# A depthwise convolution moved wholly to TensorE, by column tiles and shifted copies

## The chip, the cores and the metric

The kernel runs on one core of a Trainium2 chip. The metric is the device time of one execution in microseconds; the median of three runs is given. The program is one launch that computes three transformer blocks for 256 positions of width 1024.

## What is computed

The change touches one step of the first block, the mixer with a convolution branch. Cut to that (`S` = 256, 512 channels, 31 taps, float32):

```python
def conformer_conv(u, glu_b, dw_w, dw_b, ln_g, ln_b):
    u = u + glu_b
    a, g = jnp.split(u, 2, axis=-1)
    h = a * jax.nn.sigmoid(g)
    h = jnp.pad(h, ((0, 0), (30, 0), (0, 0)))
    h = lax.conv_general_dilated(             # depthwise: each channel with its own 31 taps
        h, dw_w[:, None, :], window_strides=(1,), padding='VALID',
        dimension_numbers=('NWC', 'WIO', 'NWC'), feature_group_count=512)
    h = layer_norm(h + dw_b, ln_g, ln_b)      # over the channels
    return jax.nn.silu(h)

# first block
h = rms_norm(x, norm1_g)
q, k, v, u = jnp.split(h @ w_in, [512, 1024, 1536], axis=-1)
q, k = rope(rms_norm(q)), rope(rms_norm(k))   # 8 heads of 64
attn = causal_attention(q, k, v)
x = x + jnp.concatenate([attn, conformer_conv(u, ...)], -1) @ w_out
x = x + swiglu(rms_norm(x))                   # width 2816
```

Two more blocks of the same size follow (other attentions, two feed-forward parts each). They are not touched.

## The kernel before, in words

**Tiling.** The 256 positions are two tiles of 128 rows (`t` = 0, 1). All weights are streamed from HBM once, in blocks of mostly 1 MB in the order of `PLAN`. `load` asks for a block into one of three `raw` buffers, on SP's queue. `split` turns it into a rounded high part on ScalarE (L242) and the remainder on VectorE (L243); the parts of four blocks fit in the pool `hl`. Each weight product is three matmuls, high by high, high by low, low by high (`mm3`, L272 to L274). Eight banks of PSUM hold four `mm` tiles, two for attention and two for transposes. `take` hands out the next block and asks for later loads and splits ahead of it.

**The first mixer** (`mixer1`). The first four weight blocks give the two halves of `u`. The gated product is transposed, and `hc[c]` holds chunk `c` of 128 channels by 30 zeros and 256 positions (L701). Then come the query block, the key block (blocks 4 to 7), the scores with softmax, lambda (a small value for the second part), the value block (8 and 9), `attend`, the norm of the convolution, and the output projection `w_out` (10 to 13). For queries and keys, ScalarE sums the squares of each head (L754), POOL takes the power (L285), VectorE does the rotary step in five operations (L531 to L535, last multiply L767), TensorE transposes (L520).

**The convolution** before is divided. Chunks 0 and 1 and the first 12 taps of chunk 2 are done on VectorE: one multiply-add of 128x256 for each tap (L731, L733), 74 in all, drawn in four portions between the other steps (`bg`). The remaining 19 taps of chunk 2 and all 31 of chunk 3 are matmuls on TensorE (L721): the stationary operand is a 128x128 diagonal of tap weights, made on the host and loaded four taps at a time on SP's queue (`dg`, two buffers, L716), the moving one a shifted slice of `hc`. The norm (L788 to L803) takes all four chunks by transposes.

**Order.** The program is written once in the order of the code, and a planner puts each engine's instructions in a fixed order: by their place in the code, but by its own estimate of when operands and buffers are ready. On the chip each engine keeps that order, and waits where something isn't ready yet. SP issues the DMAs in such an order too. Each DMA there waits until the one that used its semaphore before has landed; there are eight in turn.

Of the kernel before, what the change touches and what calls it, by code (L numbers as in the profile page):

```python
# [7 lines left out]
F32 = mybir.dt.float32  # L8
F32R = mybir.dt.float32r
BF16 = mybir.dt.bfloat16  # L10
AF = mybir.ActivationFunctionType
ALU = mybir.AluOpType
AX = mybir.AxisListType

P = 128
# [15 lines left out]
FIRST_SPLIT = 512  # L31
SLOTS = 25
E_BUFS = 9
DG_BUFS = 2
HP = 150
HP2 = 100
CONV_DVE = (31, 31, 12, 0)
BG = (10, 10, 24, 20)

# [82 lines left out]
C_DWB = 72  # L124
C_DWW = 76
# [50 lines left out]
class K:  # L176
    def __init__(self, tc, aps, pools):
        self.tc, self.nc = tc, tc.nc
        self.w, self.x_in, self.cols_in, self.rows_in, self.sh_in, self.rev_in, self.dg_in, self.out = aps
        (self.cp, self.raw, self.hl, self.sl, self.xp, self.gp, self.sm, self.psm, self.pst) = pools  # L180
        self.blk = []
        self.nload = self.nsplit = self.nuse = 0
        off = 0
        self.offs = []
        for b in PLAN:
            self.offs.append(off)
            off += P * b[3] * b[5]
        self.uid = 0
# [475 lines left out]
    def mixer1(self, nxt):  # L664
        nc = self.nc
        glu = self.row_bcast(R_GLU, 1024)
        qk = self.slot()
        for j, (r, sw) in enumerate(((R_QN, 0), (R_QN, 1), (R_KN, 0), (R_KN, 1))):
            o = qk[:, j * 64 : (j + 1) * 64]
# [19 lines left out]
        hc = [self.slot() for _ in range(4)]  # L689
        for c in range(4):  # L690
            nc.gpsimd.memset(hc[c][:, 0:30], 0.0)
        for t in range(2):
            r = self.rstd[t][:, 0:1]
            a, g = self.slot(), self.slot()
            nc.vector.scalar_tensor_tensor(a, pa[t], r, glu[:, :512], op0=ALU.mult, op1=ALU.add)
            nc.vector.scalar_tensor_tensor(g, pg[t], r, glu[:, 512:], op0=ALU.mult, op1=ALU.add)
            nc.scalar.activation(g, g, AF.Sigmoid)
            nc.vector.tensor_tensor(a, a, g, op=ALU.mult)
            tp = self.transpose4(a)
            for c in range(4):  # L700
                nc.scalar.activation(hc[c][:, 30 + t * P : 30 + (t + 1) * P], tp[:, c * P : (c + 1) * P], AF.Copy)  # L701

        w = lambda c, k: self.cols[:, C_DWW + c * 31 + k : C_DWW + c * 31 + k + 1]
        cps = {}

        def conv_pe(c):
            ks = list(range(CONV_DVE[c], 31))
            if not ks:
                return
            if not cps:  # L710
                cps["bank"] = self.mmt()
            ps = cps[c] = cps["bank"][:, (c % 2) * 256 : (c % 2 + 1) * 256]
            for g in range(0, len(ks), 4):
                dg = self.sl.tile([P, 512], F32, tag="dg", name=self.nm("dg"), bufs=DG_BUFS)
                nk = len(ks[g : g + 4])
                nc.sync.dma_start(  # L716
                    dg[:, : nk * P].rearrange("p (k m) -> p k m", k=nk),
                    self.dg_in[c, ks[g] : ks[g] + nk].rearrange("k p m -> p k m"))
                for j, k in enumerate(ks[g : g + 4]):
                    d = dg[:, j * P : (j + 1) * P]  # L720
                    nc.tensor.matmul(ps, d, hc[c][:, k : k + 256], start=(k == ks[0]), stop=(k == 30))  # L721

        acc = [self.slot()[:, :256] for _ in range(4)]

        def conv_dve():
            for c in range(4):
                a = acc[c]
                b = self.cols[:, C_DWB + c : C_DWB + c + 1]
                for k in range(CONV_DVE[c]):
                    if k == 0:  # L730
                        nc.vector.tensor_scalar(a, hc[c][:, 0:256], w(c, 0), b, op0=ALU.mult, op1=ALU.add)  # L731
                    else:
                        nc.vector.scalar_tensor_tensor(a, hc[c][:, k : k + 256], w(c, k), a, op0=ALU.mult, op1=ALU.add)  # L733
                    yield

        it = conv_dve()

        def bg(n):
            for _ in range(n):
                next(it, None)  # L740


        ops = []
        for which in range(2):
            bg(BG[which])
            ps = self.project()
            dst = [self.slot(), self.slot()]
            for t in range(2):
                r = self.rstd[t][:, 0:1]
                sq = self.slot()  # L750
                ss = self.small(8, "qss")
                for h in range(8):
                    c = slice(h * 64, (h + 1) * 64)
                    nc.scalar.activation(sq[:, c], ps[t][:, c], AF.Square, accum_out=ss[:, h : h + 1])  # L754
                r2 = self.small(1, "r2")
                nc.vector.tensor_scalar(r2, r, r, 1.0 / 64, op0=ALU.mult, op1=ALU.mult)
                ms = self.small(8, "qms")
                nc.vector.tensor_scalar(ms, ss, r2[:, 0:1], EPS, op0=ALU.mult, op1=ALU.add)
                f = self.small(8, "qf")
                self.rpow(f, ms)  # L760
                f2 = self.small(8, "qf2")
                nc.vector.tensor_scalar(f2, f, r, 0.125 if which == 0 else 1.0, op0=ALU.mult, op1=ALU.mult)
                q = self.slot()
                a = tabs[t]
                self.rope(ps[t], a[:, which * 128 : which * 128 + 64], a[:, which * 128 + 64 : which * 128 + 128], q, 8, 64)
                qv = q[:, :].rearrange("p (h d) -> p h d", d=64)
                nc.vector.tensor_tensor(qv, qv, f2[:, :].unsqueeze(2).broadcast_to([P, 8, 64]), op=ALU.mult)  # L767
                self.to_T(q, dst, t)
            ops.append(dst)
        sc = self.scores(ops[0], ops[1], lambda h: self.sh[:, H_CAUS : H_CAUS + 256])  # L770
        self.lambda_()
        bg(BG[2])
        v = self.vcopy(self.project())
        conv_pe(3)
        bg(BG[3])
        conv_pe(2)
        att = self.attend(sc, v)
        bg(999)
        for c in range(4):
            if CONV_DVE[c] == 0:  # L780
                nc.scalar.activation(acc[c], cps[c], AF.Identity, bias=self.cols[:, C_DWB + c : C_DWB + c + 1])
            elif c in cps:
                nc.vector.tensor_tensor(acc[c], acc[c], cps[c], op=ALU.add)
        cv = []
        for t in range(2):
            tp = self.tpt()
            for c in range(4):
                nc.tensor.transpose(tp[:, c * P : (c + 1) * P], acc[c][:, t * P : (t + 1) * P], self.ident)  # L788
            st, mv = self.small(6, "bst"), self.small(2, "bmv")
            nc.vector.bn_stats(st, tp)  # L790
            nc.vector.bn_aggr(mv, st)
            ve, rv = self.small(1, "bve"), self.small(1, "brv")
            nc.vector.tensor_scalar(ve, mv[:, 1:2], EPS, None, op0=ALU.add)
            self.rpow(rv, ve)
            xn = self.slot()
            nc.vector.tensor_scalar(xn, tp, mv[:, 0:1], rv[:, 0:1], op0=ALU.subtract, op1=ALU.mult)
            tp2 = self.transpose4(xn)
            s = self.slot()
            for c in range(4):
                nc.scalar.activation(  # L800
                    s[:, c * P : (c + 1) * P], tp2[:, c * P : (c + 1) * P], AF.Silu,
                    scale=self.cols[:, C_LNG + c : C_LNG + c + 1], bias=self.cols[:, C_LNB + c : C_LNB + c + 1])
            cv.append(self.split_T(s))  # L803
        part = lambda o, base: lambda t, k: tuple(a[:, (k - base) * P : (k - base + 1) * P] for a in o[t])
        self.w_out(part(att, 0), part(cv, 4), None, nxt)

# [183 lines left out]
def build(nc):  # L990
# [4 lines left out]
    rows = f("rows", [NROW], "ExternalInput")  # L995
    sh = f("sh", [P, NSH], "ExternalInput")
    rev = f("rev", [16, P, 256], "ExternalInput")
    dg = f("dg", [4, 31, P, P], "ExternalInput")
    out = f("out", [S, D], "ExternalOutput")
    PS = bass.MemoryType.PSUM  # L1000
    with TileContext(nc) as tc:
        with (
            tc.tile_pool(name="cp", bufs=1) as cp,
            tc.tile_pool(name="raw", bufs=RAW_BUFS) as raw,
            tc.tile_pool(name="hl", bufs=HL_PARTS) as hl,
            tc.tile_pool(name="sl", bufs=SLOTS) as sl0,
            tc.tile_pool(name="xp", bufs=1) as xp,
            tc.tile_pool(name="gp", bufs=1) as gp,
            tc.tile_pool(name="sm", bufs=2) as sm,
            tc.tile_pool(name="psm", bufs=MM_BUFS, space=PS) as psm,  # L1010
            tc.tile_pool(name="pst", bufs=TP_BUFS, space=PS) as pst,
        ):
            K(tc, (w, x, cols, rows, sh, rev, dg, out), (cp, raw, hl, sl0, xp, gp, sm, psm, pst)).run()

# [42 lines left out]
```

## Time and profile before

| | |
|---|---|
| median of 3 runs | 1342.89 us (1342.21 to 1345.31) |
| the profiled execution, its own time | 1345.35 us |
| its span from first to last instruction | 1343.6 us |
| TensorE's granted clock | 0.998 of full speed |
| TensorE busy | 1317.5 us |
| VectorE busy | 792.8 us |
| ScalarE busy | 677.9 us |
| HBM read | 233.44 MB, 175 GB/s over the span |

The profile shows engines as PE (TensorE's matmuls), PEld (its weight loads), DVE (VectorE), ACT (ScalarE), POOL and SP (the queue that issues DMAs). Matmuls overlap one another: a matmul's recorded length is modelled and runs into the next, so what a stream of them costs is read from the distance of their starts. "Idle before, releaser" is time in which an engine had nothing running, and what ended it.

### The profile page before, as it was taken

How to read it: one execution, taken by the hardware profiler on the slowest of the kernel's cores; microseconds unless marked ns; L12 is line 12 of the kernel's file. 1: busy time of each engine (PE TensorE's matmuls, PEld its weight loads, DVE VectorE, ACT ScalarE, POOL GpSimd, SP SyncE). 2: the span in 40 equal slices, each digit the busy share in tenths (PEclk: the TensorE clock that was granted, in tenths of full speed). 3: DMA queues.
4: the chain of work that ended last, by engine and by line, in shares of the span. 5: the costliest groups of instructions: out<-in, count | busy, mean ns of one | idle time of the engine just before them, and what ended most of it. 6: DMA issues, size and time to landing. Idle time of an engine off the chain costs nothing.

```text
span 1343.6 us, 16178 instructions
## 1 busy us (share of the span) xinstructions
PE 1317.5 (98%) x6226; PEld 1079.2 (80%) x6226; DVE 792.8 (59%) x1241; ACT 677.9 (50%) x1123; POOL 33.5 (2%) x47
## 2 busy tenths in 40 slices
PE   7989999999999999999999999999999999999998
PEld 5767888888888888777888888888888788888886
DVE  5987655545555547886665545655546544755543
ACT  5653644445544436755654444644435845744441
POOL 0100000000000000000000000000000000000000
PEclk9999999999999999999999999999999999999999
DMA  8652465554655554432465554655554452465540
GB/s 296 215 201 71 153 223 182 188 177 156 223 174 191 181 178 168 177 126 97 144 244 189 181 181 170 218 180 188 182 190 171 166 179 95 162 228 176 190 169 32
DMA packets 43470, 235.55 MB, mean 175 GB/s; under 512 B 4864, under 2 KB 13696, under 8 KB 16640
## 3 DMA queue, kind: packets, MB, share of 16 engines
q1 hardware_dynamic: 43392, 234.51, 50.4%
q8 instruction: 49, 0.80, 0.2%
q14 instruction: 29, 0.24, 0.1%
HBM read 233.44 MB, written 1.05 MB: 175 GB/s over the span
## 4 chain that ended last, share of the span: by engine, by line
PE 92%; DVE 3%; ACT 2%; DMA 1%; POOL 1%; issue 1%; SPq 0%; POOLq 0%; DVEq 0%; ACTq 0%
PE mm L274 28%; PE mm L272 28%; PE mm L273 28%; PE tp L382 2%; PE at L598 2%; PE at L565 1%; PE tp L520 1%; PE tp L308 1%; PE tp L586 1%; DMA dg<-dg 1%; PE mm L721 1%; ACT e L572 1%; DVE wl L243 1%; POOL qf L285 1%; DMA raw<-w 0%
## 5 line engine op out<-in xcount | busy, mean ns | idle before, releaser
L243 DVE TENSOR_TENSOR wl<-raw,wh 128x1024 fp32r<-128x1024 f32 (+2 forms) x430 | 514.3, 1209 | 410.1 <-ACT wh L242 397.7
L242 ACT ACTIVATE wh<-raw 128x1024 fp32r<-128x1024 f32 (+2 forms) x430 | 444.0, 1049 | 499.9 <-PE mm L274 469.8
L272 PE MATMUL mm<-wh,xh 128*128 128x512 f32 (+1 forms) x1168 | 458.7, 393 | 2.8 <-ACT wh L242 2.8
L273 PE MATMUL mm<-wl,xh 128*128 128x512 f32 (+1 forms) x1168 | 456.1, 391 | 0.5 <-DVE wl L243 0.5
L274 PE MATMUL mm<-wh,xl 128*128 128x512 f32 (+1 forms) x1168 | 456.6, 391 | 0.0
L272 PEld LDWEIGHTS mm<-wh,xh 128*128 128x128 f32 x1168 | 220.0, 188 | 48.4 <-ACT wh L242 3.6
L273 PEld LDWEIGHTS mm<-wl,xh 128*128 128x128 f32 x1168 | 219.9, 188 | 46.4 <-DVE wl L243 2.2
L274 PEld LDWEIGHTS mm<-wh,xl 128*128 128x128 f32 x1168 | 220.0, 188 | 44.3
L272 PE MATMUL mm<-wh,slot 128*128 128x512 f32 x536 | 210.3, 392 | 0.0
L273 PE MATMUL mm<-wl,slot 128*128 128x512 f32 x536 | 210.0, 392 | 0.0
L274 PE MATMUL mm<-wh,slot 128*128 128x512 f32 x536 | 209.7, 391 | 0.0
L272 PEld LDWEIGHTS mm<-wh,slot 128*128 128x128 f32 x536 | 100.7, 188 | 20.9 <-issue 1.0
L274 PEld LDWEIGHTS mm<-wh,slot 128*128 128x128 f32 x536 | 100.7, 188 | 20.7 <-DVE slot L510 0.2
L273 PEld LDWEIGHTS mm<-wl,slot 128*128 128x128 f32 x536 | 100.7, 188 | 20.0
L313 ACT ACTIVATE xh<-tp,cols 128x128 fp32r<-128x128 f32 x128 | 42.6, 369 | 31.0 <-PE tp L308 17.7
L314 DVE SCALAR_TENSOR_TENSOR xl<-tp,cols,xh 128x128 fp32r<-128x128 f32 x128 | 40.6, 346 | 20.5 <-ACT xh L313 19.3
L424 DVE SCALAR_TENSOR_TENSOR slot<-mm,rstd,slot 128x512 f32<-128x512 f32 (+1 forms) x60 | 41.7, 702 | 17.5 <-PE mm L274 17.5
L572 ACT ACTIVATE e<-e,mx 128x128 f32<-128x128 f32 (+1 forms) x80 | 35.3, 446 | 7.9 <-DVE mx L569 7.9
L423 ACT ACTIVATE slot<-mm,rstd 128x512 f32<-128x512 f32 (+1 forms) x60 | 36.5, 659 | 3.7 <-PE mm L274 3.7
L385 DVE TENSOR_TENSOR slot<-tp,slot 128x512 fp32r<-128x512 f32 (+1 forms) x60 | 35.9, 639 | 0.0
L337 ACT ACTIVATE junk<-mm 128x512 bf16<-128x512 f32 x24 | 14.4, 600 | 36.2 <-PE mm L274 36.2
L733 DVE SCALAR_TENSOR_TENSOR slot<-slot,cols,slot 128x256 f32<-128x256 f32 x71 | 32.2, 479 | 0.5
(115 smaller groups left out, 669.9 us busy)
## 6 DMA issues: line engine op xcount, KB each, us to landing
raw<-w SPq DMA_DIRECT2D x209, 1024.0 KB, 4.9
gb<-rows SPq DMA_DIRECT2D x7, 512.0 KB, 5.5
dg<-dg SPq DMA_DIRECT2D x11, 256.0 KB, 3.6
bias<-rev SPq DMA_DIRECT2D x2, 1024.0 KB, 7.4
raw<-w SPq DMA_DIRECT2D x2, 592.0 KB, 3.6
raw<-w SPq DMA_DIRECT2D x4, 256.0 KB, 6.2
raw<-w SPq DMA_DIRECT2D x2, 512.0 KB, 8.9
out<-xres SPq DMA_DIRECT2D x4, 256.0 KB, 2.0
```

Of the source, the lines that this page charges most:

```text
L242: self.nc.scalar.activation(wh[:, o], r[:, i_], AF.Copy)
L243: self.nc.vector.tensor_tensor(wl[:, o], r[:, i_], wh[:, o].bitcast(F32), op=ALU.subtract)
L272: mm(ps, xh, wh, start=start, stop=False)
L273: mm(ps, xh, wl, start=False, stop=False)
L274: mm(ps, xl, wh, start=False, stop=stop)
L313: nc.scalar.activation(xh[:, c], tp[:, j * P : (j + 1) * P], AF.Copy, scale=g)
L314: nc.vector.scalar_tensor_tensor(xl[:, c], tp[:, j * P : (j + 1) * P], g, xh[:, c].bitcast(F32), op0=ALU.mult, op1=ALU.subtract)
L385: nc.vector.tensor_tensor(hlo[:, :cw], tp, hh[:, :cw].bitcast(F32), op=ALU.subtract)
L423: nc.scalar.activation(sg[:, :cw], pg[t], AF.Silu, scale=r)
L424: nc.vector.scalar_tensor_tensor(sg[:, :cw], pu[t], r, sg[:, :cw], op0=ALU.mult, op1=ALU.mult)
L572: nc.scalar.activation(s[:, :nk], s[:, :nk], AF.Exp, bias=mx[:, h : h + 1], scale=-1.0, accum_out=sm[:, h : h + 1])
L733: nc.vector.scalar_tensor_tensor(a, hc[c][:, k : k + 256], w(c, k), a, op0=ALU.mult, op1=ALU.add)
```

## The change

All 31 taps of all four chunks become matmuls. For each chunk, 16 DMAs copy from tile to tile: for each shift `s` of 0 to 3 and each group `i` of 32 channels, the rows of that group, shifted by `s` positions, go to partitions 32`s` to 32`s`+31, columns from `i` x 284, of a tile `xc` (two buffers). A matmul then contracts 128 rows, four shifts by 32 channels, onto 32 columns: four taps of one channel group at once. Eight such groups of taps (32 with a zero tap at the end) accumulate, and the four channel groups lie in four column tiles of the array (`tile_position=(0, 32 * i)`), each writing its own 32 partitions of the bank. The stationary operands come from the host in two arrays of 1 MB (`cw`), each loaded into a `raw` buffer. ScalarE copies each chunk out with the bias. Nothing of the convolution is on VectorE; `dg` and its loads are gone. Chunks 0 and 1 stand in the code after the key block and ahead of the scores, chunks 2 and 3 after the value block, and `attend` behind the norm of the convolution.

```diff
-DG_BUFS = 2
+XC_BUFS = 2
-CONV_DVE = (31, 31, 12, 0)
-BG = (10, 10, 24, 20)
+CG = 8
+CW = 4 * CG + 252
...
             nc.gpsimd.memset(hc[c][:, 0:30], 0.0)
+            nc.gpsimd.memset(hc[c][:, 286:288], 0.0)
...
+        acc = [self.slot()[:, :256] for _ in range(4)]
+
+        def conv(c):
+            if c % 2 == 0:
+                cps["w"] = self.raw.tile([P, 2048], F32, tag="raw", name=self.nm("cw"))
+                nc.sync.dma_start(cps["w"], self.cw_in[c // 2])
                 cps["bank"] = self.mmt()
-            ps = cps[c] = cps["bank"][:, (c % 2) * 256 : (c % 2 + 1) * 256]
-            for g in range(0, len(ks), 4):
-                dg = self.sl.tile([P, 512], F32, tag="dg", name=self.nm("dg"), bufs=DG_BUFS)
...
+            xc = self.gp.tile([P, 4 * CW], F32, tag="xc", name=self.nm("xc"), bufs=XC_BUFS)
+            for s in range(4):
+                for i in range(4):
+                    nc.sync.dma_start(
+                        xc[32 * s : 32 * s + 32, i * CW : (i + 1) * CW], hc[c][32 * i : 32 * i + 32, s : s + CW])
+            wt, ps = cps["w"], cps["bank"][:, (c % 2) * 256 : (c % 2 + 1) * 256]
+            for g in range(CG):
+                for i in range(4):
+                    o = ((c % 2) * 4 + i) * 32 * CG + g * 32
+                    nc.tensor.matmul(
+                        ps[32 * i : 32 * i + 32, :], wt[:, o : o + 32],
+                        xc[:, i * CW + 4 * g : i * CW + 4 * g + 256],
+                        start=(g == 0), stop=(g == CG - 1), tile_position=(0, 32 * i))
+            nc.scalar.activation(acc[c], ps, AF.Identity, bias=self.cols[:, C_DWB + c : C_DWB + c + 1])
...
         for which in range(2):
-            bg(BG[which])
             ps = self.project()
...
+        for c in (0, 1):
+            conv(c)
         sc = self.scores(ops[0], ops[1], lambda h: self.sh[:, H_CAUS : H_CAUS + 256])
         self.lambda_()
-        bg(BG[2])
         v = self.vcopy(self.project())
-        conv_pe(3)
-        bg(BG[3])
-        conv_pe(2)
-        att = self.attend(sc, v)
-        bg(999)
...
+        for c in (2, 3):
+            conv(c)
         cv = []
...
             cv.append(self.split_T(s))
+        att = self.attend(sc, v)
```

## Rows read from the trace of the kernel before

**Rows 1.** The page's busy line (us, share, instructions) and 40 slices in tenths.
```profile
PE 1317.5 (98%) x6226; PEld 1079.2 (80%) x6226; DVE 792.8 (59%) x1241; ACT 677.9 (50%) x1123; POOL 33.5 (2%) x47
...
PE   7989999999999999999999999999999999999998
```

**Rows 2.** TensorE's timeline: start us, us from first start to last end, operation, count.
```profile
72.72 0.39 PE L274 MATMUL mm<-wh,xl 128*128 128x512 f32 x1
72.95 0.40 PE L272 MATMUL mm<-wh,xh 128*128 128x512 f32 x1
73.28 1.16 PE L565 MATMUL at<-slot,slot 64*128 64x128 f32 x16
...
77.00 1.89 PE L721 MATMUL mm<-slot,dg 128*128 128x256 f32 x8
...
85.65 1.14 PE L565 MATMUL at<-slot,slot 64*128 64x256 f32 x8
...
117.63 0.48 PE L272 MATMUL mm<-wh,slot 128*128 128x512 f32 x1
...
588.88 1.12 PE L862 MATMUL at<-slot,slot 32*128 32x256 f32 x4
```

**Rows 3.** Stretches: length, then each engine's busy us and count.
```profile
core 0: us, PE busy (x) PEld busy (x) DVE busy (x) ACT busy (x) POOL busy (x), PEclk, DMA share, GB/s
41.00:77.00 36.00, 32.48 (x159) 25.90 (x157) 31.05 (x60) 21.97 (x86) 6.74 (x5) 1.00 0.60 205
77.00:117.60 40.60, 35.18 (x197) 28.75 (x196) 33.31 (x96) 14.82 (x46) 0.46 (x1) 1.00 0.49 162
```

**Rows 4.** TensorE's waits from 41 to 118 us: total us, times, longest.
```profile
PE tp L520 <- DVE slot L767: 4.8, 4, 1.5
PE mm L721 <- DMA dg<-dg: 3.7, 3, 2.1
PE tp L586 <- ACT slot L589: 0.5, 1, 0.5
```

**Rows 5.** The convolution's matmuls, L721: ns least/median/most, first and last start us.
```profile
L721 PE MATMUL mm<-slot,dg x100: 377/379/483, 77.0 to 116.8; 128*128 128x256 f32 x100
```

**Rows 6.** The page's groups: VectorE's multiply-adds, busy us, mean ns, idle before.
```profile
L733 DVE SCALAR_TENSOR_TENSOR slot<-slot,cols,slot 128x256 f32<-128x256 f32 x71 | 32.2, 479 | 0.5
```

**Rows 7.** Stretches of the first three rope sequences: L733 alone, busy us and count.
```profile
49.77:53.75 3.98, 2.31 (x5) 1.00 0.96 316
59.51:61.70 2.19, 0.87 (x2) 1.00 0.94 393
68.33:70.26 1.93, 0.40 (x1) 1.00 0.67 280
```

**Rows 8.** ScalarE's timeline: `hc`, the bias copy, the norm's last split.
```profile
40.54 0.80 ACT L701 ACTIVATE slot<-tp 128x128 f32<-128x128 f32 x4
...
120.53 0.47 ACT L781 ACTIVATE slot<-mm,cols 128x256 f32<-128x256 f32 x1
...
134.01 0.64 ACT L509 ACTIVATE slot<-slot 128x512 fp32r<-128x512 f32 x1
```

**Rows 9.** SP's timeline; the third row is the middle one of the second's three.
```profile
2.58 1.86 SPq L221 DMA_DIRECT2D raw<-w  x4
...
57.53 16.88 SPq L221 DMA_DIRECT2D raw<-w  x3
...
65.52 0.33 SPq L221 DMA_DIRECT2D raw<-w  x1
```

**Rows 10.** The page's DMA issues: count, KB each, median us from issue to landing.
```profile
raw<-w SPq DMA_DIRECT2D x209, 1024.0 KB, 4.9
...
dg<-dg SPq DMA_DIRECT2D x11, 256.0 KB, 3.6
...
out<-xres SPq DMA_DIRECT2D x4, 256.0 KB, 2.0
```

**Rows 11.** The stretch of the value block: L274 alone, busy us and count.
```profile
62.50:77.00 14.50, 6.08 (x16) 3.01 (x16) 1.00 0.34 110
```

More of the change, by code (lines that the diff above doesn't have):

```diff
@@ L178, in __init__ @@
         self.tc, self.nc = tc, tc.nc
-        self.w, self.x_in, self.cols_in, self.rows_in, self.sh_in, self.rev_in, self.dg_in, self.out = aps
+        self.w, self.x_in, self.cols_in, self.rows_in, self.sh_in, self.rev_in, self.cw_in, self.out = aps
         (self.cp, self.raw, self.hl, self.sl, self.xp, self.gp, self.sm, self.psm, self.pst) = pools
@@ L701, in mixer1 @@
                 nc.scalar.activation(hc[c][:, 30 + t * P : 30 + (t + 1) * P], tp[:, c * P : (c + 1) * P], AF.Copy)
-        w = lambda c, k: self.cols[:, C_DWW + c * 31 + k : C_DWW + c * 31 + k + 1]
         cps = {}
[L706 to L710, printed above, removed]
-                cps["bank"] = self.mmt()
-            ps = cps[c] = cps["bank"][:, (c % 2) * 256 : (c % 2 + 1) * 256]
-            for g in range(0, len(ks), 4):
-                dg = self.sl.tile([P, 512], F32, tag="dg", name=self.nm("dg"), bufs=DG_BUFS)
[L715 to L740, printed above, removed]
+        acc = [self.slot()[:, :256] for _ in range(4)]
[3 more added lines that the diff above has]
+                nc.sync.dma_start(cps["w"], self.cw_in[c // 2])
+                cps["bank"] = self.mmt()
+            xc = self.gp.tile([P, 4 * CW], F32, tag="xc", name=self.nm("xc"), bufs=XC_BUFS)
[12 more added lines that the diff above has]
+            nc.scalar.activation(acc[c], ps, AF.Identity, bias=self.cols[:, C_DWB + c : C_DWB + c + 1])
@@ L769, in mixer1 @@
             ops.append(dst)
+        for c in (0, 1):
+            conv(c)
         sc = self.scores(ops[0], ops[1], lambda h: self.sh[:, H_CAUS : H_CAUS + 256])
         self.lambda_()
-        bg(BG[2])
         v = self.vcopy(self.project())
-        conv_pe(3)
-        bg(BG[3])
-        conv_pe(2)
-        att = self.attend(sc, v)
-        bg(999)
[L779 to L783, printed above, removed]
+        for c in (2, 3):
+            conv(c)
         cv = []
@@ L997, in build @@
     rev = f("rev", [16, P, 256], "ExternalInput")
-    dg = f("dg", [4, 31, P, P], "ExternalInput")
+    cw = f("cw", [2, P, 2048], "ExternalInput")
     out = f("out", [S, D], "ExternalOutput")
@@ L1012, in build @@
         ):
-            K(tc, (w, x, cols, rows, sh, rev, dg, out), (cp, raw, hl, sl0, xp, gp, sm, psm, pst)).run()
+            K(tc, (w, x, cols, rows, sh, rev, cw, out), (cp, raw, hl, sl0, xp, gp, sm, psm, pst)).run()
 def kernel(**inputs):
@@ L1048 @@
     rev = np.ascontiguousarray(rel[:, np.maximum(191 + i - k, 0)])
-    dg = np.zeros((4, 31, P, P), np.float32)
-    dg[:, :, np.arange(P), np.arange(P)] = a["dw_w"][0].reshape(31, 4, P).transpose(1, 0, 2)
+    taps = np.zeros((4, 4, 32, 4 * CG), np.float32)
+    taps[:, :, :, :31] = a["dw_w"][0].reshape(31, 4, 4, 32).transpose(1, 2, 3, 0)
+    cw = np.zeros((4, 4, 32, 4, CG, 32), np.float32)
+    j = np.arange(32)
+    for s in range(4):
+        cw[:, s, j, :, :, j] = taps.reshape(4, 4, 32, CG, 4)[:, :, :, :, s].transpose(2, 0, 1, 3)
+    cw = np.ascontiguousarray(cw.reshape(2, 2, P, 4 * CG * 32).transpose(0, 2, 1, 3)).reshape(2, P, 2048)
     nc = bacc.Bacc("TRN2", target_bir_lowering=False, num_devices=1)
@@ L1054 @@
         nc,
-        [{"w": w, "x": np.ascontiguousarray(a["x"][0]), "cols": cols, "rows": rows, "sh": shape_consts(), "rev": rev, "dg": dg}],
+        [{"w": w, "x": np.ascontiguousarray(a["x"][0]), "cols": cols, "rows": rows, "sh": shape_consts(), "rev": rev, "cw": cw}],
         core_ids=[0],
```

## The prediction

> **What bounds the kernel now.** I read the page's busy line and slices first. TensorE is busy 98% of the span and nine tenths or more in nearly every slice [rows 1]. So time is won or lost where TensorE's own work or its idle time changes. The convolution belongs to the first mixer, and TensorE's timeline gives its place: its first matmul follows the value block's products at 77.0 us, and the output projection starts at 117.63 [rows 2]. From 41 to 77 us VectorE is busy 31.05 of 36.0 us and TensorE 32.48, from there to 117.6 VectorE 33.31 of 40.6 and TensorE 35.18 [rows 3]. The table of waits then says what TensorE's idle time there consists of: 4.8 us for the four last multiplies of the rotary step on VectorE (L767), 3.7 us for three loads of `dg`, 0.5 us for a copy on ScalarE (L589); 9.0 us together [rows 4]. That is all that better cover can give back. The rest has to come from TensorE's own instructions.
>
> **Removed.** On TensorE, 50 matmuls of 128x256 in fp32, which the trace shows as 100 records [rows 5]. The recorded 379 ns is a modelled length that overlaps the next one; the spacing counts: eight records in 1.89 us [rows 2], (1.89 - 0.38) / 7 = 0.216 us each, so 0.432 us a matmul and 100 x 0.216 = 21.6 us. On VectorE, 71 multiply-adds, 32.2 us busy [rows 6], and their few first and joining operations. VectorE is not the bound, so these count only through L767. Between the rope's operations stand five, two and one of them in the first three rope sequences, some 0.4 us each [rows 7]: 2.0 us go ahead of the first wait, and the longest of the four is 1.5 [rows 4], and what the first sequence gains the later ones inherit, since the next block's squares wait on ScalarE behind the copies of the transposed rows. I let three of the four waits go and keep one of the longest size, for the last now stands at the head of the softmax chain: 4.8 - 1.3 = 3.5 us. Ends: 0 and 4.8. The `dg` waits, 3.7 us, go with their loads. Eleven loads of 192 to 256 KB leave the DMA queue.
>
> **Added on TensorE.** Four chunks of 8 groups of 4 matmuls, 128 in all, each contracting 128 rows (four taps by 32 channels) onto 32 columns, with 256 columns streaming as before. If nothing runs side by side, one costs what the removed one costs: 128 x 0.432 = 55.3 us. If the four column tiles stream at once, a group costs one: 32 x 0.432 = 13.8 us. No matmul of before uses column tiles; the nearest rows are the tiles by rows. The scores of heads in alternating halves (64 rows) take 1.14 us for eight records of 256 columns, (1.14 - 0.38) / 7 = 0.109 us each, half of 0.216: two tiles run fully at once. The index products, all on one row tile at that place, show the opposite: four records in 1.12 us, about the 0.216 us of a full array again [rows 2]. So a narrow tile alone gains nothing and a second one costs nothing. I take this over to four column tiles, since it is the nearest row, and add about 1.2 us for changing from full array to tiles and back: the first score product starts at 73.28 us, 0.33 after the weight product before it, where two weight products stand 0.23 apart [rows 2]; some ten such changes would make it. So 15 us; ends 13.8 and 55.3.
>
> [...]
>
> **Added elsewhere.** ScalarE: four copies with bias instead of one, 0.47 us each [rows 8], 1.4 us more where it has 25.8 of 40.6 us free [rows 3]: nothing. POOL: four memsets more, nothing. SP: 64 copies between tiles in place of 11 loads, and two weight loads of 1 MB. Four issues in a row took 1.86 us [rows 9], 0.465 each, so 7.4 us a chunk and 29.8 us in all. The queue is free for that: three weight loads span 16.9 us in waiting for their buffers [rows 9]. `hc` is whole at 41.3 us [rows 8], so the copies of chunks 0 and 1 can be out by about 57. A landing took 2.0 us (output), 3.6 (`dg`) and 4.9 (1 MB) at the median [rows 10]; I use 2 to 5 for the small copy, whose kind the trace doesn't have.
>
> **Moved.** Convolution 0 and 1 now stand ahead of scores, lambda and the value projection, 2 and 3 behind it, the layer norm ahead of `attend`. The weights of the convolution take one of the three `raw` buffers. Weight blocks 10 and 11 are asked for before it, so it gets about the buffer that block 12 got at 65.52 us [rows 9], and lands near 70. Blocks behind it come one buffer later; they are due for the output projection (12 and 13 for its second half) and the FFN after 128 us, so I cost that at nothing, and at a landing, 4.9 us [rows 10], if that cover is gone. Lambda's load on SP comes behind 32 copies; VectorE's product for it, in order, would hold the first norm behind it, but lambda stands ahead of chunks 2 and 3 in the program: nothing. Two buffers hold the copies: those of chunk 2 wait on SP for the last matmul of chunk 0, those of chunk 3 for chunk 1, and each weight load queued behind them on SP waits too; TensorE, whose queue is in order, waits with everything behind the matmul. From conv 0 finished near 74: 7.4 + 2 to 5 gives chunk 2 at 83 to 86, chunk 3 at 91 to 94. The value projection (48 matmuls after 62.5 us, sixteen of each kind [rows 11], 11 us by the 0.23 spacing) will be about done by then; what lies between as cover are the second half of the scores, the transposes of the probabilities and their products with the values. The norm took from 120.53 to 134.65 us [rows 8] and may now run beside `attend` and the first half of the output projection.
>
> New waits on TensorE I put at 5 us. Below, 0, if that work covers everything. Above, 12: both later chunks wait for a full set of copies (7.4 + 3 each, 21 us) with some 9 us of other work in front. I take less than the middle, because projection and convolution 0 and 1 can be shifted into the softmax chain.
>
> **Sum.** -21.6 + 15 - 3.7 - 3.5 + 5 = -8.8 us. Best: -21.6 + 13.8 - 9.0 = -16.8. The profiled execution took 1345.35 us, its span 1343.6 with 1.75 around it, so 1336.6 on its own scale. It is 2.46 us over the median of the three runs, 1342.89; the measured kernel will be read against that, so 1342.89 - 8.8 = 1334. Behind the mixer nearly every slice has TensorE at nine tenths or more [rows 1], so what is won there stays.
>
> **Rivals.**
> 1. *Column tiles don't overlap.* Each matmul streams alone, 55.3 us in place of 21.6, +33.7; all 9.0 us of waits are covered by the long convolution, +25, so 1368. For it: the index products, where a tile without a partner takes full time, and that rows show only tiles whose operands lie on different partitions, while these four read the same 128. Against it: the tiles write different columns and no data passes between them, as in the scores. It decides from a speed-up below 55.3 / (21.6 + 9.0) = 1.8: slower under that.
> 2. *Only neighbours overlap*, the second record of one with the first of the next: 0.216 us a matmul, 27.6 us; +6.0 - 8.5 + 2 = 0, 1343. For it: each fp32 matmul is two records, and the scores, with two tiles, cannot tell this from four at once by their spacing alone.
> 3. *The copies come late.* Tiles overlap, but 64 copies feed 128 matmuls through two buffers, and an order fixed ahead puts the matmuls where they were thought ready: waits of 13 us in place of 5, about -1, 1342. For it: TensorE already waited for `dg` three times with two buffers. Against it: the first half of the copies has 20 us of lead.
>
> [...]
>
> **Chances.** Forecast 0.59, rival 1 0.18, rival 2 0.11, rival 3 0.12. Forecast's own range: 1326 to 1341. The range for 8 in 10 takes in rivals 2 and 3 and leaves rival 1 out: 1324 to 1350. Two runs of this kernel can be told apart from about 0.2%, 2.7 us. Faster: 0.57 + 0.02 + 0.05 = 0.64; within it: 0.02 + 0.07 + 0.04 = 0.13; slower: 0.18 + 0.02 + 0.03 = 0.23.
>
> **What would show it.** Matmul records of 32 columns starting in fours within a few hundredths, the fours 0.216 us apart, 14 to 16 us in all: forecast. Starts 0.216 apart singly: rival 1 with 256 records; in twos: rival 2. TensorE's waits for copies of `xc` above 10 us: rival 3. The waits on L767 should shrink to about one, and the output projection start near 109 us in place of 117.6. A convolution of 14 us with no gain at all would prove the accounting by TensorE wrong.

## The result: slower by 1.1%, and the profile after

The changed kernel takes 1358.78 us (median of 4 runs, 1358.4 to 1360.93) where the kernel before took 1342.67 beside it (1342.21 to 1345.31). The ratio is 1.0111, with an interval of 1.0095 to 1.0126. The forecast was 1334 in a range of 1324 to 1350, so it was wrong in sign. The profiled execution took 1358.84 us, its span 1356.7.

The page first, its busy line and TensorE's 40 slices, which answer to [rows 1]:

```profile
PE 1320.1 (97%) x6382; PEld 1072.6 (79%) x6382; DVE 763.5 (56%) x1166; ACT 679.1 (50%) x1126; POOL 33.4 (2%) x51
...
PE   7796999999999999999999999999999999999998
```

VectorE lost its multiply-adds as planned. Of the 40 slices, the second and the fourth are lower than before (7 for 9, 6 for 9) and the third is higher (9 for 8); behind the mixer they are the same. The stretches of [rows 3], with a third up to the new start of the output projection:

```profile
41.00:77.00 36.00, 27.28 (x158) 19.30 (x156) 24.58 (x42) 18.05 (x80) 6.56 (x4) 0.91 0.52 176
77.00:117.60 40.60, 39.80 (x351) 26.53 (x350) 10.79 (x41) 20.15 (x53) 0.00 (x0) 1.00 0.51 167
117.60:131.80 14.20, 4.13 (x18) 3.01 (x17) 5.62 (x12) 5.58 (x12) 1.11 (x2) 0.58 0.26 104
```

TensorE is busy 5.2 us less in the first stretch than before, 4.6 more in the second, and then comes a stretch of 14.2 us that did not exist: busy 4.13 us, the granted clock 0.58. The projection that started at 117.63 us [rows 2] starts at 131.79. TensorE's table of waits, from 41 to 135 us, answers to [rows 4]:

```profile
PE tp L521 <- DVE slot L752: 8.7, 4, 5.7
PE tp L521 <- DVE slot L774: 5.7, 2, 2.9
PE tp L521 <- DVE slot L623: 3.7, 1, 3.7
PE mm L722 <- DMA xc<-slot: 0.7, 1, 0.7
PE mm L273 <- ACT slot L510: 0.7, 1, 0.7
```

19.5 us in place of 9.0. The lines are the rope's last multiply (L752, before L767), the norm of the convolution (L774), the multiply at the end of `attend` (L623), the copies and a split. The copies, for which the prediction had kept 5 us, are the smallest entry. Where the waits lie is in TensorE's timeline (start, length, instruction, idle before it and who ended that):

```profile
62.06 0.66 PE L521 MATMUL tp<-sh,slot 128*128 128x128 f32 x4 [1.61 <-DVE slot L752]
...
68.47 1.09 PE L521 MATMUL tp<-sh,slot 128*128 128x128 f32 x4 [5.75 <-DVE slot L752]
...
101.63 3.66 PE L722 MATMUL mm<-xc,cw 128*32 128x256 f32 x64
...
117.33 0.28 PE L766 MATMUL tp<-sh,slot 128*128 128x128 f32 x1
...
120.37 1.09 PE L521 MATMUL tp<-sh,slot 128*128 128x128 f32 x4 [2.77 <-DVE slot L774]
121.25 1.06 PE L766 MATMUL tp<-sh,slot 128*128 128x128 f32 x4
...
125.26 1.09 PE L521 MATMUL tp<-sh,slot 128*128 128x128 f32 x4 [2.94 <-DVE slot L774]
...
130.02 1.08 PE L521 MATMUL tp<-sh,slot 128*128 128x128 f32 x4 [3.67 <-DVE slot L623]
131.79 0.79 PE L273 MATMUL mm<-wh,slot 128*128 128x512 f32 x1 [0.69 <-ACT slot L510]
```

The reader is to see three things. A chunk of the convolution, 64 records, takes 3.66 us: all four column tiles stream at once. The longest single wait stands at 62.7 us in the rope, where the value block's products stood before [rows 11]; now these come only after 78 us. And from 117.6 us to the projection TensorE does a handful of transposes, one link of a chain after another; four of them take 1.09 us at a granted clock of 0.50 (120.37 us), where 0.66 was enough at 1.00 (62.06 us). VectorE's timeline shows what the chain is made of:

```profile
117.64 0.70 DVE L768 BATCH_NORM_STATS2 bst<-tp 128x6 f32<-128x512 f32 x1 [12.95 <-PE tp L766]
...
124.31 0.80 DVE L774 TENSOR_SCALAR slot<-tp,bmv,brv 128x512 f32<-128x512 f32 x1
...
129.19 0.68 DVE L623 TENSOR_TENSOR slot<-at,rs 128x512 f32<-128x512 f32 x1
```

The products that L623 reads were finished before 117.6. It runs at 129.19 because VectorE's fixed order has it behind the norm of both tiles. SP's timeline, [rows 9], and the page's line for the copies, [rows 10]:

```profile
44.90 0.59 SPq L716 DMA_DIRECT2D xc<-slot  x1
53.02 0.34 SPq L222 DMA_DIRECT2D raw<-w  x1
55.89 0.33 SPq L711 DMA_DIRECT2D cw<-cw  x1
56.27 20.79 SPq L716 DMA_DIRECT2D xc<-slot  x31
77.58 0.81 SPq L222 DMA_DIRECT2D raw<-w  x2
86.62 0.33 SPq L711 DMA_DIRECT2D cw<-cw  x1
```
```profile
xc<-slot SPq DMA_DIRECT2D x64, 35.5 KB, 1.9
```

The first 32 copies are issued by 77 us, not by 57: two of SP's weight loads waited in front of all but the first until 55.9, and 31 copies took 20.79 us, 0.67 each.

### The profile page after: what moved, and what is told of

Its sections match the earlier page's. It is cut to its first block, busy times and chain, and to the rows that moved or that the text cites. A ratio compares the mean times of both kernels' runs of the same rounds, so it can differ in the third digit from the quotient of the medians.

```text
span 1356.7 us, 16505 instructions
## 1 busy us (share of the span) xinstructions
PE 1320.1 (97%) x6382; PEld 1072.6 (79%) x6382; DVE 763.5 (56%) x1166; ACT 679.1 (50%) x1126; POOL 33.4 (2%) x51
## 4 chain that ended last, share of the span: by engine, by line
PE 90%; DVE 3%; ACT 3%; SPq 1%; DMA 1%; issue 1%; POOL 1%; DVEq 0%; POOLq 0%; ACTq 0%
PE mm L275 27%; PE mm L274 27%; PE mm L273 27%; PE tp L383 2%; PE at L599 1%; PE tp L521 1%; PE at L566 1%; PE tp L309 1%; SPq L716 1%; PE mm L722 1%; PE tp L587 1%; DVE wl L244 1%; ACT e L573 1%; DMA raw<-w 1%; ACT slot L739 0%
## 5 line engine op out<-in xcount | busy, mean ns | idle before, releaser
L244 DVE TENSOR_TENSOR wl<-raw,wh 128x1024 fp32r<-128x1024 f32 (+2 forms) x430 | 514.1, 1208 | 418.5 <-ACT wh L243 405.6
L274 PE MATMUL mm<-wl,xh 128*128 128x512 f32 (+1 forms) x1168 | 456.2, 391 | 0.4 <-DVE wl L244 0.4
L274 PEld LDWEIGHTS mm<-wl,xh 128*128 128x128 f32 x1168 | 219.7, 188 | 46.0 <-DVE wl L244 1.6
L274 PE MATMUL mm<-wl,slot 128*128 128x512 f32 x536 | 210.8, 393 | 0.0
L274 PEld LDWEIGHTS mm<-wl,slot 128*128 128x128 f32 x536 | 101.3, 189 | 20.0
L521 PE MATMUL tp<-sh,slot 128*128 128x128 f32 x136 | 23.1, 298 | 19.0 <-DVE slot L752 8.7
L521 PEld LDWEIGHTS tp<-sh,slot 128*128 128x128 f32 x136 | 17.0, 153 | 25.8 <-issue 19.5
```

The source lines that it names most:

```text
L244: self.nc.vector.tensor_tensor(wl[:, o], r[:, i_], wh[:, o].bitcast(F32), op=ALU.subtract)
L274: mm(ps, xh, wl, start=False, stop=False)
L521: self.nc.tensor.transpose(tp[:, j * P : (j + 1) * P], src[:, j * P : (j + 1) * P], self.ident)
```

## The experiments

Each run stands beside runs of the kernel before on the same chip, whose medians were 1344.85, 1344.74, 1344.31 and 1344.53 us for runs 1 to 4, 5 to 8, 9 to 12 and 13 to 15. Theory A: `attend` behind the norm of the convolution makes the hole ahead of the projection. Theory B: the convolution's bank, one of four `mm` tiles, keeps the value projection from filling the rope waits (filler here means matmuls that are ready to run while a chain of other work isn't). Theory C: the copies come late. Theory D: the column tiles themselves are slow.

**1. The bank** (B). The first bank comes from the attention banks:

```diff
-                cps["bank"] = self.mmt()
+                cps["bank"] = self.mmt() if c else self.att()
```

> The changed kernel with one edit: the bank of chunks 0 and 1 comes from the attention pool instead of the four mm tiles. Theory A (the bank of the convolution keeps the value projection from being the filler of the rope waits, 62.7 to 68.5 us): the waits of TensorE on the rope's last multiply fall from 8.7 us to under 5, the clock there goes back to full, the output projection starts 7 to 9 us earlier, about 1350 us. Theory B (the rope chain itself has become late, or the place of chunks 0 and 1 in the code displaces the projection): no change, 1357 to 1360.

1357.23 us, 1.0089 (1.0074 to 1.0104). TensorE's waits on the rope and on the softmax:

```profile
PE tp L521 <- DVE slot L752: 2.9, 3, 1.2
PE tp L587 <- ACT slot L590: 1.7, 1, 1.7
PE tp L587 <- ACT e L573: 1.4, 2, 0.9
```

The rope's waits fell from 8.7 to 2.9 us and the value projection is filler again, so B names the cause of that wait. But the softmax now has one attention bank, and new waits stand behind it: 3.1 us in these two lines, and 0.6 on the bias copy (L726). The copies' 0.7 us is gone. 5.8 + 0.7 - 3.7 leaves 2.8 us, and the projection starts at 128.71 us, 3.1 earlier (1.0111 to 1.0089).

**2. The place of `attend`** (A).

```diff
+        att = self.attend(sc, v)
         cv = []
...
             cv.append(self.split_T(s))
-        att = self.attend(sc, v)
```

> The changed kernel with attend put back ahead of the norm of the convolution, nothing else. Theory A (TensorE stands empty from 117.6 to 131.8 us because attend's transposes are queued behind the norm's and the norm waits for chunk 3): the first half of the output projection fills the norm's waits, 9 to 12 us less, about 1348 us. Theory B (chunk 3 is late by its copies, and whatever stands behind it waits): 3 us less at most, 1355 or more.

1346.62 us, 1.0012 (1.0003 to 1.0022): of the 1.11% by which the change is slower, 0.99 come back by one moved line, some 13 of 15 us. L623 is gone from TensorE's waits and the norm's share is 0.2 us.

**3. Both.**

> Both edits, bank and attend. If the two holes are separate, the gains add: 16 to 20 us less than the changed kernel, 1339 to 1343, no better than level with before. If the second hole only takes in what the first gives back, 1348 to 1350. If the column tiles, their mode changes or the copies were the cost, 1355 or more.

1343.74 us, 0.9994 (0.9984 to 1.0004): no loss, and not the gain either. Chunk 2 ran only from 99.8 us; its copies were issued from 86 to 99. Before that TensorE had little but the softmax chain's work, at a granted clock of 0.78 from 78 to 101 us.

**4. Column tiles in turn** (D). The two loops of the convolution change places, so that eight matmuls on one tile follow each other:

```diff
-            for g in range(CG):
-                for i in range(4):
+            for i in range(4):
+                for g in range(CG):
```

> The changed kernel with the two loops of the convolution's matmuls exchanged: eight matmuls of one column tile, then eight of the next, the same 128 matmuls. If only different column tiles run side by side and the queue is in order, a chunk takes 64 x 0.216 = 13.8 us in place of 3.66, some 40 us more in all, about 1395 to 1400 us. If matmuls are reordered between tiles, a chunk stays under 5 us and the time within 3 us of 1359.

1381.85 us (one run). TensorE's timeline, the four chunks:

```profile
69.98 13.69 PE L722 MATMUL mm<-xc,cw 128*32 128x256 f32 x64
...
86.59 11.50 PE L722 MATMUL mm<-xc,cw 128*32 128x256 f32 x64
...
113.95 11.50 PE L722 MATMUL mm<-xc,cw 128*32 128x256 f32 x64
...
128.44 11.50 PE L722 MATMUL mm<-xc,cw 128*32 128x256 f32 x64
```

The same instructions take 11.50 us in place of 3.66 (13.69 in the first chunk, where the clock was 0.84), 0.18 us a record in place of 0.057. So neighbours must sit on different tiles, the change's order does that, and D is out: the tiles cost what was forecast.

**5. The order alone, in the kernel before** (A against everything else). Diagonals, VectorE taps and `dg` loads stay; only `attend` goes behind the norm:

```diff
         conv_pe(2)
-        att = self.attend(sc, v)
         bg(999)
...
             cv.append(self.split_T(s))
+        att = self.attend(sc, v)
```

> The kernel before, with its diagonal matmuls and VectorE taps as they were, and one thing changed: attend stands behind the norm of the convolution, where the change put it. If that place is itself the cause (the output projection's first half reads attend's output, so the norm's chain and attend's chain then run one behind the other with TensorE idle, as in the 14.2 us hole at 117.6 to 131.8 us of the changed kernel), it costs here too what moving it back gained there: +10 to +14 us, 1354 to 1359 us. Rival: the place only hurts together with column tiles, whose results come late; then this is within 3 us of the kernel before, 1342 to 1348.

1359.85 us, 1.0118 (1.0101 to 1.0135), a little over A's range: a loss as large as that of the change, without any of its convolution. TensorE's waits:

```profile
PE tp L520 <- DVE slot L795: 5.7, 2, 2.9
PE tp L520 <- DVE slot L767: 4.8, 4, 1.4
PE tp L520 <- DVE slot L622: 3.7, 1, 3.7
```

The first and the third are, to a tenth, the two entries of the changed kernel (L774, L623). The projection starts at 133.50 us.

**6. The copies on another queue** (C against A). `nc.sync.dma_start` of the copies becomes `nc.gpsimd.dma_start`, nothing else.

> The changed kernel with the 64 shifted copies issued from GpSimd's queue and nothing else changed (bank and attend's place as the change has them). If the loss is the copies standing in SyncE's queue behind weight loads (0.633 us apart there, chunk 3's copies complete near 109.6 us), most of it comes back: 1343 to 1349 us. If the loss is the place of attend behind the norm, the hole ahead of the output projection stays whatever the copies do, and only the few us by which the convolution ends earlier come back: 1351 to 1358 us.

1354.26 us, 1.0071 (1.0056 to 1.0086), inside A's range. The hole stays; the chunks end at 110.3 us instead of 116.4, and the projection starts at 127.43.

**7 and 8. Order, bank and queue together,** with the first bank from the attention banks (7) or the two transpose banks (8: `self.tpt()` for `self.att()`).

> The changed kernel with three edits: the first convolution bank taken from the attention banks, attend ahead of the norm (with these two it took 1343.7 us, 0.9994 of the kernel before), and now the 64 copies on GpSimd's queue. If the late copies on SyncE's queue are what ate the rest (chunk 2 stood at 99.8 to 105.7 us because its copies were issued from 86 to 99 us), chunks 2 and 3 now fit between the other work and the time falls to 1331 to 1338 us. If TensorE's stretch between 76 and 100 us is set by the softmax chain alone, the copies change nothing: 1342 to 1345 us.

> As the run with attend ahead of the norm and the copies on GpSimd's queue, but the first convolution bank taken from the two transpose banks, not from the attention banks. If the missing attention bank was what delayed the scores' second half and drew out the softmax chain, this is the shortest: TensorE has the value projection as filler of the rope waits and both attention banks for the scores, 1329 to 1336 us. If one transpose bank for two chunks costs as much (each transpose then waits for the eviction of the one before), it is no better than with the attention bank: 1338 to 1346 us.

1342.31 us, 0.9983 (0.9974 to 0.9992), and 1344.51, 0.9999 (0.999 to 1.0009): both missed the range that I hoped for and lie in that of the rival. In run 7 TensorE waits 5.62 us for the first rope, where it waited 1.45 before. VectorE's timeline and POOL's say why:

```profile
54.48 0.23 DVE L747 TENSOR_SCALAR qf<-qf,rstd 128x8 f32<-128x8 f32 x1 [6.04 <-POOL qf L286]
```
```profile
41.49 4.11 POOL L716 DMA_DIRECT2D xc<-slot  x8 [25.68 <-ACT slot L703]
...
51.77 0.99 POOL L716 DMA_DIRECT2D xc<-slot  x2 [0.66 <-DMA xc<-slot]
52.78 1.67 POOL L286 TENSOR_TENSOR qf<-qms,mhalf 128x8 f32<-128x8 f32 x1
```

After the first eight copies the next six go out one or two at a time as others land, and the power of the query norm stands behind them in POOL's order. So POOL's order, like SP's, holds something that TensorE needs. In run 8 the rope waits are 7.8 us, and those on copies 3.8.

**9, 10 and 11. Two queues.** Chunks 0 and 1 on SP's queue, 2 and 3 on POOL's (9 with the attention bank, 10 with the transpose bank) or on ScalarE's (11, transpose bank):

```diff
-                    nc.sync.dma_start(
+                    (nc.sync if c < 2 else nc.gpsimd).dma_start(
```

> First convolution bank from the attention banks, attend ahead of the norm, and the copies on two queues: those of chunks 0 and 1 on SyncE's as in the change, those of chunks 2 and 3 on GpSimd's. With all 64 on GpSimd's queue the power of q's norm (a GpSimd instruction) stood behind copies that waited there, VectorE had it 6.0 us late and TensorE waited 5.6 us for the first rope. If that was what ate the gain of earlier copies, it goes here and the time falls to 1336 to 1340 us. Rival: SyncE's copies of chunk 1 (until 78 us) and the stretched softmax chain set the stretch from 62 to 101 us whatever chunks 2 and 3 do: 1341 to 1345 us.

> The same two queues, with the first convolution bank taken from the two transpose banks, so that the scores keep both attention banks and the value projection both of its tiles. If the bank is the other half of the loss, TensorE is busy from 54 us to the output projection and this one is the shortest of all: 1333 to 1338 us. If one transpose bank costs what the attention bank cost, it is as the run with the attention bank, 1336 to 1345 us.

> As the run with the transpose bank and two queues, but the copies of chunks 2 and 3 on ScalarE's queue instead of GpSimd's. ScalarE does the exponentials of the softmax in that stretch: if 32 issues there take the place of its work (some 0.5 us each by GpSimd's record, 0.6 us by SyncE's), probabilities come up to 16 us late and it takes 1340 to 1350 us; if an issue costs ScalarE next to nothing, the time is that of the run on GpSimd's queue.

1345.13 us, 1.0004 (0.9994 to 1.0013); 1341.24, 0.9975 (0.9965 to 0.9985); 1349.82, 1.0031 (1.0019 to 1.0044). In 9 the rope wait is 2.8 us again, as meant, but TensorE waits 2.4 us for the bias copy of chunk 2 and the clock is 0.85 and 0.90 in the two stretches from 78 to 117.6 us (cut at 101): the time is at the upper end of the rival's range. In 10 the transpose bank pays 3.9 us against 9, though the time lies in the range of the second case and not of the first; beside 4.5 us for the rope, the wait that is left is 5.5 us on chunk 2's copies. Run 11 is inside the range of its first case. ScalarE's order shows the price of issuing there:

```profile
81.25 9.18 ACTq L716 DMA_DIRECT2D xc<-slot  x10
90.48 0.47 ACT L726 ACTIVATE slot<-tp,cols 128x256 f32<-128x256 f32 x1 [9.07 <-DMA xc<-slot]
```

**12. All chunks behind the value projection,** bank as the change has it, `attend` first, two queues.

> Attend ahead of the norm, the two queues, the bank as the change has it (one of four projection tiles), but all four chunks of the convolution behind the value projection, as the kernel before had its convolution. The value projection then fills the rope waits without any bank trade. Copies of chunks 2 and 3 can start only when chunks 0 and 1 are done (two buffers), near 97 us, and 32 issues of 0.5 us end near 113 us: if that tail is on the path, 1340 to 1347 us; if attend's matmuls cover it, 1334 to 1339 us.

1348.79 us, 1.0032 (1.002 to 1.0043), above both ranges: TensorE waits 5.6 us, until 102.93, on chunk 2's copies, which POOL issues only from 90.50 to 100.94 us; chunk 3's follow from 102.65 to 110.5.

**13, 14 and 15. A third buffer.** 13 makes room (the four results in two slots, 23 slots for 25) and changes nothing else of run 10; 14 adds the buffer; 15 also takes chunk 2's copies to SP (`c < 3`).

```diff
-XC_BUFS = 2
+XC_BUFS = 3
```

> The best arrangement so far (attend ahead of the norm, first bank from the transpose banks, copies of chunks 0 and 1 on SyncE's queue and of 2 and 3 on GpSimd's; 0.9975 of the kernel before) with the four convolution results packed in two slots and the pool of slots cut from 25 to 23. No theory expects a gain; if the two slots are needed somewhere in the later layers, it is slower by what they cost: 1340 to 1345 us. It is the control for a third buffer, which takes this memory.

> The control with a third buffer for the shifted copies and nothing else. If TensorE's wait of 5.5 us on chunk 2's copies is the wait for chunk 0's buffer, those copies now go out some 15 us earlier, the wait goes, the clock stays up behind it, and it is 4 to 7 us shorter than the control. If GpSimd's queue itself is slow (32 copies took it from 81.6 to 106.6 us), chunk 2 is in time but chunk 3 stays where it is: within 2 us of the control.

> As the run with the third buffer, but chunk 2's copies too are on SyncE's queue, so GpSimd's holds 16 copies only. SyncE then issues them behind chunk 1's, from about 78 us, and the second weights of the convolution and the weights of the output projection stand behind or among them. If GpSimd's queue was the brake, it is 2 to 4 us shorter than the run with the third buffer; if SyncE's queue with the weights is, the weights come late and it is 1 to 6 us longer.

1341.42 us, 0.9976 (0.9964 to 0.9988); **1334.89, 0.9934 (0.9917 to 0.9952)**; 1345.18, 1.0006 (0.9995 to 1.0018). The buffer alone is worth 6.5 us, as its theory said: POOL issues chunk 2's first copies at 63.91 us, where 13 has 81.62. In 13, TensorE's timeline has chunk 2 like this:

```profile
97.14 2.95 PE L723 MATMUL mm<-xc,cw 128*32 128x256 f32 x18 [4.90 <-DMA xc<-slot]
```

and in 14 so, with the projection behind it:

```profile
93.93 1.81 PE L723 MATMUL mm<-xc,cw 128*32 128x256 f32 x18 [0.18 <-DMA cw<-cw]
...
108.91 0.48 PE L273 MATMUL mm<-wh,slot 128*128 128x512 f32 x1
```

In 15 only one of chunk 2's 16 copies goes out ahead of the second weights of the convolution, which wait on SP until 85.14; the others stand behind them. SP's timeline:

```profile
79.42 1.26 SPq L717 DMA_DIRECT2D xc<-slot  x1
85.14 0.33 SPq L712 DMA_DIRECT2D cw<-cw  x1
85.52 9.95 SPq L717 DMA_DIRECT2D xc<-slot  x12
```

It is 10.3 us slower than 14, more than the 1 to 6 expected: TensorE waits 3.8 us on copies, and the clock is 0.88 and 0.76 in the same two stretches from 78 to 117.6. Run 14 is the version that beats both kernels. Its page and its stretches up to the projection:

```profile
PE 1309.6 (98%) x6382; PEld 1068.5 (80%) x6382; DVE 762.4 (57%) x1166; ACT 678.1 (51%) x1126; POOL 49.4 (4%) x83
```
```profile
41.00:77.00 36.00, 31.46 (x157) 24.75 (x159) 25.76 (x55) 20.47 (x87) 12.14 (x16) 1.00 0.55 185
77.00:108.90 31.90, 30.28 (x355) 20.89 (x348) 10.51 (x31) 17.56 (x48) 10.32 (x22) 0.95 0.74 244
```

From 41 us to the projection: 67.9 us, TensorE busy 31.46 + 30.28 = 61.7 and idle 6.2. Before: 76.6 us, busy 67.7, idle 8.9 [rows 3]. So 5.9 us less work and 2.8 less idle time, 8.7 together.

## Why the prediction was wrong

**The step that failed** is the last sentence of "Moved": the norm "may now run beside `attend` and the first half of the output projection". The diff does the opposite. Before, the projection started at 117.63 [rows 2] and the norm ran from 120.53 to 134.65 [rows 8]: the projection, whose first half reads only `attend`, covered those 14 us. The stretch from 117.6 us in the kernel before has TensorE busy 13.93 of 14.40 us at full clock, where the changed kernel has 4.13 of 14.20:

```profile
117.60:132.00 14.40, 13.93 (x72) 11.15 (x72) 10.89 (x20) 7.90 (x12) 1.12 (x2) 1.00 0.22 73
```

With `attend` behind the norm, nothing is ready while the norm runs, and `attend`'s own end (multiply, transposes, split) follows it. The order written in the code was read, and what it takes away as cover was not asked. Run 5 puts the price at 15.1 us (1359.85 against 1344.74), run 2 gives some 13 back; the two entries L774 and L623, 9.4 us, are the same in the change and in run 5 (L795 and L622 there). The forecast missed by 24.8 us (1358.78 against 1334): the order is some 13 of them, and the two paragraphs on the rope and on the copies hold most of the rest.

**New waits, +5 us, put on the copies.** Copies cost 0.7 us in the changed kernel. The term held the wrong waits: measured are 9.4 us of norm and `attend`, and the lower clock, 0.58 in the hole and 0.89 from 131.8 to 156 us.

**Rope waits, -3.5 us.** They rose from 4.8 to 8.7, because the filler went: the convolution's bank is one of the four `mm` tiles and the value projection needs two (run 1: 8.7 to 2.9 by the bank alone). The prediction costed the moved convolution in time and in `raw` buffers, not in PSUM. The term fails even without that. VectorE's chain was to be 2.0 us shorter in the first rope sequence. From its scale `qf` to the last multiply it took 3.98 us [rows 7] and takes 3.68 (49.23 to 52.91) in the changed kernel, for remainders of weight splits (L244) now stand where the multiply-adds stood:

```profile
50.04 1.22 DVE L244 TENSOR_TENSOR wl<-raw,wh 128x1024 fp32r<-128x1024 f32 x1
...
51.77 1.22 DVE L244 TENSOR_TENSOR wl<-raw,wh 128x1024 fp32r<-128x1024 f32 x1
52.91 0.68 DVE L752 TENSOR_TENSOR slot<-slot,qf 128x512 f32<-128x512 f32 x1
```

Run 14, with the filler back, still has all four waits, 4.5 us, so 0.3 is gained and not 3.5:

```profile
PE tp L521 <- DVE slot L753: 4.5, 4, 1.7
PE tp L587 <- ACT e L573: 1.4, 1, 1.4
```

**The copies' issue, 0.465 us each and out by 57.** They took 0.67 each and were out at 77, since that rate came from four loads with nothing in front of them, and SP's two waiting loads were not put ahead of them. In the changed kernel this is hidden by the other loss; with the order mended, late copies cost time beside the bank, as rival 3 said in kind. From run 2 (order alone) by run 10 (with bank and queues) to run 14 (with the third buffer) the ratio goes from 1.0012 by 0.9975 to 0.9934, 0.78% or 10.5 us; the copies' part that was tested alone is the buffer, 6.5 us. SP's copies landed in 1.9 us at the median, a little under the 2 to 5 of the prediction. They were issued 0.67 us apart, so the landings overlapped; what came late was the issue.

**What was right.** -21.6 + 15 for the matmuls: a chunk in one piece takes 3.66 us, four 14.6. In run 14 the busy time of TensorE is 5.9 us lower up to the projection, and 7.9 over the whole span (1317.5 to 1309.6). Rivals 1 and 2 are out by the same rows: 55.3 and 27.6 us were their prices. Run 4 adds that a column tile without a partner cost 0.18 us a record (11.50 / 64), not the 0.216 in rival 1's price, and that a chunk with its tiles in turn took 11.50 / 3.66 = 3.1 times as long as with four side by side. The sum of -8.8 us describes run 14 (the projection at 108.91 us where "near 109" was written), not the kernel that was predicted: its tiles were accounted for, its order was not. Even for run 14 it is partly luck. The rope gave 0.3 us and not 3.5, and the new waits, on the softmax and on the convolution's weights, are 1.6 us and not 5: two errors that nearly cancel.

One thing stays open. Bank and queues were not changed one at a time with the order mended, except the attention bank (run 3, 2.9 us less than run 2 by the medians), and the waits don't tell what each stretch at a lower clock cost; how the 10.5 us divide between bank and queues ahead of the buffer isn't shown.

## What to carry to other kernels

When a diff moves a step, ask of each long chain which matmuls covered it before and whether they can still start: here a chain of 14 us cost TensorE half a microsecond of waiting under a ready product, and some 15 us in front of it. Count the banks of PSUM that a moved step holds as you count time, for they decide what can fill a wait (run 1: 8.7 us of rope waits became 2.9 by the bank alone). Many small copies are paid in the place that they take in an engine's order (in run 7 VectorE waited 6.04 us for a power that stood behind 14 of them on POOL); look at what each queue has behind them before choosing it, and try one buffer more: the third was worth 6.5 us here. And the time that was freed on VectorE went to what stood next in its order, so that the chain of the first rope took 3.68 us after 3.98: look at what that is before counting it as a shorter chain.

## What the runs showed of the hardware

- Four column tiles of a 128-row contraction in fp32 stream at once if neighbouring matmuls sit on different tiles (64 records in 3.66 us); eight matmuls in a row on one tile, then the next, take 11.50 us at the same granted clock, 1.00, 3.1 times as long.
- The hole was paid twice: over its 14.2 us, with TensorE busy for 4.13, the granted clock was 0.58, and four transposes took 1.09 us at 0.50 in place of 0.66 at 1.00; the first weight products behind it, at 0.50 from 131.79 to 135 us, started 0.42 to 0.59 us apart, not 0.23.
- One issue of a 36 KB copy between tiles is recorded with 0.59 us on SP (median of the changed kernel), 0.50 on POOL (single issues of run 7) and 0.51 to 0.65 on ScalarE (single issues of run 11). In a row they took 0.67 each on SP (31 in 20.79 us) and 0.51 on POOL for the first eight (4.11 us), then waits for landings came between. ScalarE's first ten took 9.18 us, and its next work waited 9.07 us for them.
